# First expert's token rows by comparisons and a product; the largest expert last, with the last norm of all tokens beside it

## The chip, the cores and the metric

One Trainium2 chip, one of its cores. The metric is the device time of one execution in microseconds (us). The kernel before takes 1973.52 us, the median of three runs (1973.03 to 1980.09). Engines are named as in the profile: PE multiplies matrices, PEld loads its weights, DVE works on vectors, ACT applies functions, POOL (GpSimd) and SP issue transfers, and POOL also does some vector work.

## The reference, cut to what matters

A decoder layer on 1024 tokens of 1024 columns: an input projection, a gated mixing unit and a dilated attention beside it, an output projection, a layer norm (its result is `h`), a router that gives each token 4 of 32 experts, the experts, and a last layer norm. The part that the change touches:

```python
logits = hf @ w_router + b_router
top_vals, top_idx = lax.top_k(logits, TOP_K)          # 4 of 32 experts for each token
gates = softmax(top_vals)
# for each expert e, on its tokens xb:
g = minimum(xb @ w_gate[e] + b_gate[e], 7)
u = clip(xb @ w_up[e] + b_up[e], -7, 7)
act = (u + 1) * (g * sigmoid(1.702 * g))
out = (act @ w_down[e] + b_down[e]) * gate            # added to the token's row of y
x = layer_norm(alpha * h + y, ln2_g, ln2_b)
```

## The kernel before, in words

**Front.** Projections, gating and attention run first. Then the output projection goes tile by tile, 8 tiles of 128 tokens: `mix` (L536) gives a tile's rows, `logits` its 32 router values, `route` its four experts. `route` makes the 0/1 rows `sel` with four operations (L606, L608), gets each token's place in its expert's list from a product (L610, L612), picks the four places with four more operations (L622), and writes token number and gate to `table` in DRAM with four indirect writes on POOL's queue (L632). `settle` applies the first norm and stores `h` to `hs` in DRAM; `start` stores the starting value of the last sum to `ys`. Tile t is settled and started during tile t+1; the last two tiles wait until `rank` has sorted the experts by their number of tokens (`perm` L558, `order` L561). `follow` orders their instructions behind that.

**Experts.** Experts are taken by rank, in the order of the list `ORDER`; `CAPS` gives the token slots of each rank (256 for rank 0, 64 for rank 31). Ranks with over 128 slots are wide, the others narrow. The order before begins 0, 30, 15, 29, 1, 28, 14, 27 and ends 6, 18, 9, 17, 7, 16, 8, 31. `fetch` loads the expert's part of `table` (`tg`, L737) on SP's queue and gathers its rows of `hs` (`xg`, L749) on POOL's; `prepare` transposes them on PE (L758). Weights come in twelve pieces of 1 MB (L781, SP's queue, five buffers), each split into a high and a low part by ACT (L120) and DVE (L121), two pieces ahead of PE. SP's order is the program's; other engines' instructions are placed by the scheduler when they are ready in its model, earlier lines first. For each expert PE does gate and up of the first half (4 pieces), then the *down* product of the expert before (4 pieces), then gate and up of the second half. Products are L830 (wide) and L821 (narrow). `finish` transposes back for wide experts (L930), scales by the gate (ACT L931, L923), and adds the rows to `ys` by an indirect accumulating write on POOL's queue (L933). Loads 2 to 6 of the weights wait until the first expert's tokens have come.

**End.** After the last expert the rows of the last norm's scale and shift are spread by PE (L977), a loop handles tokens beyond the slots (none here), and 8 tiles of `ys` are loaded (SP, L1047), normalised in three groups `TAILS` (statistics on DVE for tiles 0 and 2, on ACT for the others; L1068 and L1069 on DVE) and stored (L1070).

Of the kernel before, what the change touches and what calls it, by code (L numbers as in the profile page):

```python
# [21 lines left out]
T = 1024  # L22
D = 1024
# [19 lines left out]
ORDER = [r for n in range(8) for r in (n, 30 - 2 * n, 15 - n, 29 - 2 * n)][:31] + [31]  # L43
# [9 lines left out]
TAILS = [(0, 1), (2, 3, 4), (5, 6, 7)]  # L53
ONDVE = (0, 2)
# [23 lines left out]
def layer(tc, i, out):  # L78
# [9 lines left out]
    table = dp.tile([E * SLOTS, 2], I32, name="table")  # L88

# [9 lines left out]
    ln2 = const("ln2", [P, 2, KT], i["ln2_T"])  # L99
# [3 lines left out]
    ovf = cp.tile([1, 2 * MAXOV + 1], I32, name="ovf")  # L103
# [25 lines left out]
    def left_over(pool, bank):  # L129
# [35 lines left out]
        V.tensor_copy(ovf[:, 2 * MAXOV:2 * MAXOV + 1], pn[:, 0:1])  # L165

# [377 lines left out]
    sels, writes = [], []  # L544

    def rank():
# [11 lines left out]
        V.tensor_scalar(perm[:64], ie[:64], kc[:, 1:2], None, op0=OP.is_equal)  # L558
        po = bank("mm", (P, E))
        TE.matmul(po[:1], ecol, perm[:E], start=True, stop=True)  # L560
        return V.tensor_copy(order, po[:1])  # L561
# [36 lines left out]
    def route(t, x, mu, rs, lg):  # L598
# [6 lines left out]
        sel = A.tile([P, 2, E], BF, name="sel", bufs=2)  # L605
        V.tensor_scalar(sel[:, 0], ie, xf[:, 0:1], None, op0=OP.is_equal)  # L606
        for j in range(1, TOPK):
            V.scalar_tensor_tensor(sel[:, 0], ie, xf[:, j:j + 1], sel[:, 0], op0=OP.is_equal, op1=OP.add)  # L608
# [10 lines left out]
        junk = A.tile([P, E], FT, name="junk", bufs=2)  # L619
        dst = A.tile([P, TOPK], I32, name="dst", bufs=2)  # L620
        for j in range(TOPK):
            V.scalar_tensor_tensor(junk, ie, xf[:, j:j + 1], pp, op0=OP.is_equal, op1=OP.mult,  # L622
                                   accum_out=pos[:, j:j + 1])
        mark = V.scalar_tensor_tensor(dst, xf, float(SLOTS), pos, op0=OP.mult, op1=OP.add)
        g4 = A.tile([P, TOPK], FT, name="g4", bufs=2)
# [14 lines left out]
    def settle(t, x, mu, rs, mark):  # L640
        h = big("pt", 3)
        follow(V.scalar_tensor_tensor(h, x, mu[:, 0:1], ln_g, op0=OP.add, op1=OP.mult), mark)
        V.scalar_tensor_tensor(h, h, rs, ln_b, op0=OP.mult, op1=OP.add)
        S.dma_start(out=hs[t * P:t * P + P], in_=h)
        return h

    def start(t, h, lg, sel, den, mark):
# [9 lines left out]
        y = big("pr", 2)  # L657
# [12 lines left out]
    def settle_all(mark=None):  # L670
        rest = []
        for t, x, mu, rs, lg, sel, den, m in done:
            rest.append((t, settle(t, x, mu, rs, mark or m), lg, sel, den, mark or m))
        for r in rest:
            start(*r)
        done.clear()

    for t in range(NT):
        for step in "ablscdr":
# [14 lines left out]
    settle_all(rank())  # L694
# [14 lines left out]
    with (tc.tile_pool(name="c", bufs=1, reuse_waits="tile") as C,  # L709
# [20 lines left out]
        def fetch(r):  # L730
# [6 lines left out]
            SP.dma_start(out=tg, in_=tv[ds(e, 1), 0:nb].rearrange("a b p c -> p (a b) c"))  # L737
# [5 lines left out]
            for q in range(nb):  # L743
# [6 lines left out]
                                              in_offset=bass.IndirectOffsetOnAxis(ap=k.idx, axis=0))  # L750
# [27 lines left out]
        def load(r, c):  # L778
# [4 lines left out]
            if 1 < len(loads) <= RAWS + 1:  # L783
                tc.add_manual_dep(w.ins, first.ins.name, mybir.DependencyInfo(
# [6 lines left out]
        def downs(r):  # L791

            return (8, 10, 9, 11) if r == ORDER[-1] else (8, 9, 10, 11)

        pieces, ready, loads = [], [], []
        for n, r in enumerate(ORDER + [None]):
            pieces += [(r, c) for c in (0, 2, 1, 3)] if r is not None else []
            pieces += [(ORDER[n - 1], c) for c in downs(ORDER[n - 1])] if n else []
# [98 lines left out]
        def down(b):  # L897
# [3 lines left out]
            for c in downs(b.r):  # L901
# [4 lines left out]
                if c == downs(b.r)[2 if b.r == ORDER[-1] else 0]:  # L906
# [29 lines left out]

        bhl = C.tile([P, 2, D], FR, name="bhl")
# [12 lines left out]
        with tc.manual_schedule(engines={mybir.EngineType.SP}):  # L950
# [3 lines left out]
            prepare(b)  # L954
            last, extra = None, left_over(C, bank)
            for n, r in enumerate(ORDER):
# [11 lines left out]
                gu(b, 1, lambda: (finish(), turn(b, 0)))  # L968
                last, b = b, nxt
            down(last)()  # L970


    ZP = top.enter_context(tc.tile_pool(name="zpsum", bufs=1, space=PSUM))
# [150 lines left out]
```

## Time and profile before

| | us |
|---|---|
| median of three runs | 1973.52 |
| the profiled execution's own time | 1973.29 |
| its span, first to last instruction | 1971.4 |
| PE busy | 1844.5 (94%) |
| DVE busy | 1548.3 (79%) |
| ACT busy | 1315.8 (67%) |

A row of a timeline gives the start (us from the span's start), the duration, engine, line, operation, what is written and read, shapes and how many instructions are merged; in brackets the idle time ahead of it and what ended it. `SPq` and `ACTq` are transfers issued on those queues. A row of the chain of waits gives start, duration, and what the time was spent in.

### The profile page before, as it was taken

The page shows a single profiled execution, that of the slowest core. Times are in us where ns is not written, and L with a number is a line of the kernel's source. Part 1 is how long each engine was busy: PE and PEld are TensorE (multiplying, and loading weights), DVE is VectorE, ACT ScalarE, POOL GpSimd, SP SyncE. Part 2 cuts the span into 40 slices and gives each one's busy share as a digit, 9 for nine tenths or more (in the row PEclk, how much of TensorE's full clock was granted, in tenths as well). Part 3 has the DMA queues.
Part 4 walks back from the last instruction along what each step waited for, and adds up shares of the span by engine and source line. Part 5 has one row for each costly group of instructions (what it writes and reads, how often), then busy time and mean ns, then how long its engine had stood idle before and what let it go on. Part 6 is the DMA issues. An engine that isn't in the chain of part 4 may idle for free.

```text
span 1971.4 us, 32268 instructions
## 1 busy us (share of the span) xinstructions
PE 1844.5 (94%) x12232; PEld 1519.5 (77%) x12232; DVE 1548.3 (79%) x2169; ACT 1315.8 (67%) x1731; POOL 312.1 (16%) x200
## 2 busy tenths in 40 slices
PE   8999998989959999999999999999999999999981
PEld 7687786678747768888887888888888888888861
DVE  5754747667759778778888789898988988989895
ACT  5533526552337677678777778778877887887873
POOL 2111110213330112020111112011111111201110
PEclk9999999989969999999999999999999999999996
DMA  6111101242268898889899899999999999999884
GB/s 202 50 44 35 40 25 36 69 152 97 87 234 317 285 325 305 304 298 371 302 300 351 296 332 322 364 328 317 377 308 334 360 330 348 327 359 348 307 282 176
DMA packets 93054, 495.01 MB, mean 251 GB/s; under 512 B 20880, under 2 KB 21440, under 8 KB 43744
## 3 DMA queue, kind: packets, MB, share of 16 engines
q1 hardware_dynamic: 75856, 442.48, 60.7%
q0 software_dynamic: 14736, 42.04, 8.7%
q10 hardware_dynamic: 2304, 8.39, 1.1%
q8 instruction: 98, 1.61, 0.3%
q14 instruction: 60, 0.49, 0.1%
HBM read 456.59 MB, written 36.27 MB: 250 GB/s over the span
## 4 chain that ended last, share of the span: by engine, by line
PE 53%; DMA 8%; DVE 6%; issue 2%; ACT 2%; POOL 1%; SPq 0%; POOLq 0%; ACTq 0%; DVEq 0%
PE b L830 28%; PE b L821 22%; DMA raw<-in_w_moe 4%; DVE wl L121 3%; DMA ys<-o,tg 3%; PE b L758 2%; ACT wh L120 2%; PE b L930 1%; PE b L844 1%; DVE y L1069 1%; DMA bias<-in_b_guT 0%; DVE y L1068 0%; DMA y<-ys 0%; POOL table L632 0%; DVE tw L867 0%
## 5 line engine op out<-in xcount | busy, mean ns | idle before, releaser
L121 DVE TENSOR_TENSOR wl<-raw,wh 128x2048 bf16<-128x2048 f32 (+1 forms) x385 | 874.8, 2284 | 155.0 <-ACT wh L120 153.6
L120 ACT ACTIVATE wh<-raw 128x2048 fp32r<-128x2048 f32 (+1 forms) x394 | 742.4, 1893 | 153.0 <-DMA raw<-in_w_moe 46.8
L830 PE MATMUL b<-xw,wh 128*128 128x280 f32 (+13 forms) x1920 | 326.4, 324 | 0.0
L830 PEld LDWEIGHTS b<-xw,wh 128*128 128x128 f32 x1920 | 297.8, 190 | 9.5
L821 PE MATMUL b<-wh,xt 128*128 128x512 f32 x1056 | 283.4, 409 | 0.1
L821 PEld LDWEIGHTS b<-wh,xt 128*128 128x128 f32 x1056 | 198.9, 189 | 51.0 <-DVE xt L121 1.0
L830 PEld LDWEIGHTS <-wl 128*128 128x128 bf16 x2880 | 209.0, 97 | 18.1 <-issue 5.1
L749 POOL DMA_INDIRECT xg<-hs,tg x47 | 78.1, 1662 | 743.6 <-PE b L758 264.8
L933 POOL DMA_INDIRECT ys<-o,tg x47 | 110.2, 2344 | 424.8 <-ACT o L931 153.0
L830 PE MATMUL b<-aw,wh 128*128 128x280 f32 (+13 forms) x960 | 160.0, 321 | 0.7 <-DVE aw L121 0.7
L830 PE MATMUL b<-xbw,wl 128*128 128x140 bf16 (+13 forms) x1920 | 153.4, 237 | 2.2 <-DVE wl L121 2.2
L830 PEld LDWEIGHTS b<-aw,wh 128*128 128x128 f32 x960 | 147.7, 188 | 5.5 <-DVE aw L121 0.9
L821 PE MATMUL b<-wh,at 128*128 128x512 f32 x528 | 147.6, 421 | 0.0
L821 PE MATMUL b<-wl,xbt 128*128 128x512 bf16 x544 | 130.1, 382 | 0.0
L865 ACT ACTIVATE sb<-b 128x140 f32<-128x140 f32 (+13 forms) x240 | 71.8, 313 | 79.1 <-PE b L830 72.4
L821 PEld LDWEIGHTS b<-wh,at 128*128 128x128 f32 x528 | 99.9, 192 | 26.2 <-issue 0.6
L821 PEld LDWEIGHTS <-xbt 128*128 128x128 bf16 x544 | 48.0, 98 | 67.6 <-issue 19.5
L867 DVE SCALAR_TENSOR_TENSOR tw<-b,bias,sb 128x140 f32<-128x140 f32 (+13 forms) x240 | 83.8, 389 | 11.3 <-ACT sb L865 10.6
L830 PE MATMUL b<-abw,wl 128*128 128x140 bf16 (+13 forms) x960 | 77.1, 237 | 2.4 <-ACT abw L880 1.7
L124 PE MATMUL mm<-xh,wh 128*128 128x512 f32 x160 | 69.2, 432 | 10.3 <-DVE ks L359 6.9
L821 PE MATMUL b<-wl,abt 128*128 128x512 bf16 x272 | 72.4, 390 | 6.2 <-ACT abt L760 5.7
L124 PE MATMUL mm<-vh,xh 128*128 128x256 f32 x256 | 72.6, 284 | 0.6 <-DVE ql L344 0.6
(364 smaller groups left out, 2804.8 us busy)
## 6 DMA issues: line engine op xcount, KB each, us to landing
raw<-in_w_moe SPq DMA_DIRECT2D x384, 1024.0 KB, 7.2
raw<-in_w_in SPq DMA_DIRECT2D x18, 512.0 KB, 3.7
raw<-in_w_out SPq DMA_DIRECT2D x8, 512.0 KB, 3.5
t<-in_x SPq DMA_DIRECT2D x8, 512.0 KB, 4.2
hs<-pt ACTq DMA_DIRECT2D x8, 512.0 KB, 3.6
ys<-pr ACTq DMA_DIRECT2D x8, 512.0 KB, 2.6
y<-ys SPq DMA_DIRECT2D x8, 512.0 KB, 7.3
out<-y SPq DMA_DIRECT2D x8, 512.0 KB, 2.6
```

Of the source, the lines that this page charges most:

```text
L120: S.activation(hi, src, AF.Copy)
L121: by.tensor_tensor(lo, src, hi.bitcast(FT), op=OP.subtract)
L124: TE.matmul(o, ah, bh, start=start, stop=False)
L749: k.got = G.indirect_dma_start(out=k.x[:k.n], out_offset=None, in_=hs, in_offset=bass.IndirectOffsetOnAxis(ap=k.idx, axis=0))
L758: TE.transpose(tp[:, j], src(j), ident[:n, :n])
L821: TE.matmul(o, a, b, start=first and q == 0, stop=kq == 1 and q == len(every) - 1)
L830: TE.matmul(o, a, b, start=kq == 0 and j == 0, stop=kq == 1 and j == 3)
L844: TE.matmul(p, b.oh, bhl[:, m, half * 512:half * 512 + 512], start=True, stop=False)
L865: S.activation(x2[:, :n], p[f][:, n:2 * n], AF.Copy)
L867: V.scalar_tensor_tensor(t[:, f * n:f * n + n], p[f][:, :n], b.bias[:, c:c + 1], x2[:, :n], op0=OP.add, op1=OP.add)
L930: TE.transpose(tp[:k.n, f], t[:, f, k.q * P:k.q * P + k.n], ident)
L933: G.indirect_dma_start(out=ys, out_offset=bass.IndirectOffsetOnAxis(ap=k.idx, axis=0), in_=k.o[:k.n], in_offset=None, compute_op=OP.add)
```

## The change

- **Order.** Rank 0, the largest, goes last: 1, 30, 15, 29, 2, 28, 14, 27, ... 7, 18, 9, 17, 8, 16, 31, 0.
- **First rows.** The first expert's tokens are no longer read from `table`: `first_rows` picks the expert's places of all 1024 tokens (`place`, one more operation per tile in `route`), compares them with 256 slot numbers (16 comparisons of 128 columns on DVE), and gets the token numbers from products with (1, token base). Its `tg` is loaded later, behind the second and third weight pieces. The first weight load waits for the last store of `hs`. `start` of the last tile follows `first_rows`.
- **Router.** The four operations for `sel` become one broadcast comparison and a reduction, and so do the four for `pos`. The tile before the last is settled during the last one.
- **End.** Before the second half of the last expert its predecessor's rows are written; then the tiles of `ys` are loaded, normalised one by one and stored on POOL's queue beside the last expert's work. The last expert's *down* keeps the tokens in place (`down_last`), adds to its gathered rows of `ys`, and writes the normalised rows over `out` by indirect writes.
- **Scale and shift rows** go to DRAM by 16 small transfers at the very start, and are read back as rows.
- The loop for tokens beyond the slots stands within an outer loop that runs once if there are any, and then all tiles are normalised again.

```diff
-ORDER = [r for n in range(8) for r in (n, 30 - 2 * n, 15 - n, 29 - 2 * n)][:31] + [31]
+ORDER = [r for n in range(7) for r in (n + 1, 30 - 2 * n, 15 - n, 29 - 2 * n)] + [8, 16, 31, 0]
...
-ONDVE = (0, 2)
+ONDVE = (0, 3, 6)
...
-    ln2 = const("ln2", [P, 2, KT], i["ln2_T"])
+        for n in range(2):
+            for k in range(KT):
+                G.dma_start(out=rowd[n:n + 1, k * P:k * P + P].rearrange("n p -> p n"), in_=i["ln2_T"][:, n, k:k + 1])
...
+    def first_rows():
+        pr = bank("po", (P, E))
+        TE.matmul(pr, perm[:E, ORDER[0]:ORDER[0] + 1].to_broadcast([E, P]), ident[:E, :E], start=True, stop=True)
+        own = spare[:, NT * E + 256:2 * NT * E + 256].rearrange("p (t e) -> p t e", t=NT)
+        V.tensor_tensor(own, place, pr.unsqueeze(1).to_broadcast([P, NT, E]), op=OP.mult)
+        at = A.tile([P, NT], FT, name="at")
+        V.tensor_reduce(at, own, axis=AX.X, op=OP.add)
+        for q in range(2):
+            m = big(("kb", "ql0")[q], 1, BF).rearrange("p (t s) -> p t s", t=NT)
+            ps = bank("s", (P, 2))
+            for t in range(NT):
+                V.tensor_scalar(m[:, t], slot[:, q * P:q * P + P], at[:, t:t + 1], None, op0=OP.is_equal)
+                TE.matmul(ps, m[:, t], who[:, t], start=t == 0, stop=t == NT - 1)
+            mark = V.tensor_scalar(rows0[:, q:q + 1], ps[:, 0:1], float(T), ps[:, 1:2], op0=OP.add, op1=OP.add)
+        return mark
...
-        h = big("pt", 3)
+        h = big("pt", 3) if t + 2 < NT else big(f"ks{t + 2 - NT}")
...
-            elif step == "s" and t + 1 < NT:
+            elif step == "s":
                 settle_all()
+                if t + 1 < NT:
+                    start_all()
...
-    settle_all(rank())
+    done[0] = (*done[0][:-1], rank())
+    settle_all()
+    start_all(first_rows())
...
-                                              in_offset=bass.IndirectOffsetOnAxis(ap=k.idx, axis=0))
+                                              in_offset=bass.IndirectOffsetOnAxis(
+                                                  ap=k.idx if r != ORDER[0] else rows0[:k.n, q:q + 1], axis=0))
...
-            if 1 < len(loads) <= RAWS + 1:
-                tc.add_manual_dep(w.ins, first.ins.name, mybir.DependencyInfo(
+            if len(loads) <= RAWS + 1:
+                tc.add_manual_dep(w.ins, (first if len(loads) > 1 else norms[-1]).ins.name, mybir.DependencyInfo(
...
+        def last_norm(b):
+            rows = C.tile([P, 2, D], FT, name="bhl")
+            for n in range(2):
+                G.dma_start(out=rows[:, n], in_=rowd[n:n + 1].to_broadcast([P, D]))
+            ...
+            held = {t: tile_of(t) for t in range(6)}
+            for k in b.parts:
+                G.indirect_dma_start(out=k.y, out_offset=None, in_=ys,
+                                     in_offset=bass.IndirectOffsetOnAxis(ap=k.idx, axis=0))
+            yield
+            for t in range(NT):
+                y = held.pop(t) if t in held else tile_of(t)
+                ...
+                normed(y, y, mv[:, 0:1], rsqrt(C, mv[:, 1:2], 1, "rz"), rows)
+                G.dma_start(out=out[t * P:t * P + P], in_=y)
+                yield
+
+        def down_last(b, step):
+            ...
+                if kq:
+                    for k, p, s in zip(b.parts, ps[half], st):
+                        V.scalar_tensor_tensor(k.y[:, d], p, k.gate, k.y[:, d], op0=OP.mult, op1=OP.add)
+                        V.bn_stats(s[:, half], k.y[:, d])
+                step()
+                step()
+            mv = C.tile([P, 2, 2], FT, name="mv", bufs=3)
+            for k, s in zip(b.parts, st):
+                G.indirect_dma_start(out=ys, out_offset=bass.IndirectOffsetOnAxis(ap=k.idx, axis=0),
+                                     in_=k.y, in_offset=None)
+                V.bn_aggr(mv[:, k.q], s)
+            ...
+            for k in b.parts:
+                z = C.tile([P, D], FT, name="tw", bufs=3)
+                normed(z, k.y, mv[:, k.q, 0:1], rs[:, k.q:k.q + 1], b.rows)
+                G.indirect_dma_start(out=out, out_offset=bass.IndirectOffsetOnAxis(ap=k.idx, axis=0),
+                                     in_=z, in_offset=None, bounds_check=T - 1, oob_is_err=False)
...
+            finish()
+            norms = last_norm(b)
+            next(norms)
+            gu(b, 1, lambda: next(norms))
+            next(norms)
+            next(norms)
+            down_last(b, lambda: next(norms, None))
```

## Rows read from the trace of the kernel before

**Rows 1.** The profile's first part: busy us, share of the span, instructions of each engine.
```profile
PE 1844.5 (94%) x12232; PEld 1519.5 (77%) x12232; DVE 1548.3 (79%) x2169; ACT 1315.8 (67%) x1731; POOL 312.1 (16%) x200
```

**Rows 2.** Stages: length, then PE, PEld, DVE, ACT, POOL busy; clock, DMA share, GB/s.
```profile
555.00:565.00 10.00, 0.00 (x0) 0.00 (x0) 3.84 (x13) 1.91 (x1) 3.21 (x3) 0.50 0.48 134
...
596.70:618.40 21.70, 21.70 (x131) 18.08 (x130) 20.35 (x22) 17.17 (x20) 2.32 (x1) 1.00 0.89 351
...
690.00:800.00 110.00, 105.93 (x567) 82.07 (x566) 87.44 (x75) 80.71 (x83) 18.68 (x8) 0.97 0.91 324
...
1500.00:1600.00 100.00, 99.69 (x728) 83.21 (x727) 87.39 (x87) 83.77 (x103) 16.94 (x8) 1.00 0.97 343
```

**Rows 3.** The chain of waits, 530 to 580 us, and the first expert product (timeline, PE).
```profile
546.09 4.93 POOL table L632
...
561.88 2.60 POOL xg L749
...
564.79 5.27 DMA xg<-hs,tg
...
572.64 5.47 PE L830 MATMUL b<-xw,wh 128*128 128x512 f32 x16
```

**Rows 4.** Timeline of DVE and POOL, 544 to 556 us.
```profile
544.50 0.23 DVE L558 TENSOR_SCALAR perm<-ie,kc 64x32 f32<-64x32 f32 x1
544.81 0.97 POOL L632 DMA_INDIRECT table<-pay,dst  x1 [0.52 <-DVE perm L558]
545.24 2.46 DVE L642 SCALAR_TENSOR_TENSOR pt<-t,mean,tab 128x1024 f32<-128x1024 f32 x2
...
553.60 1.80 POOL L938 MEMSET bhl<- 64x2048 f32 x1
...
555.79 0.29 DVE L776 TENSOR_SCALAR oh<-onesr,perm 128x128 fp32r<-128x128 f32 x1
```

**Rows 5.** The profile's transfers: KB each, median us from issue to landing.
```profile
hs<-pt ACTq DMA_DIRECT2D x8, 512.0 KB, 3.6
```

**Rows 6.** Timeline of POOL and DVE near the start.
```profile
3.14 0.59 POOL L92 DMA_DIRECT2D ln<-in_ln_T  x1
...
16.98 0.42 DVE L307 TENSOR_TENSOR ws<-ws,le 128x256 f32<-128x256 f32 x1 [0.67 <-DMA ws<-in_sgu_wT]
```

**Rows 7.** PE near the end: timeline, and of the chain the row of 128 products.
```profile
1878.63 0.40 PE L844 MATMUL b<-bhl,oh 128*128 128x512 f32 x1
...
1886.47 13.69 PE b L830 x128
...
1903.85 1.91 PE L930 MATMUL b<-ident,tw 128*128 128x128 f32 x16
...
1925.24 1.28 PE L821 MATMUL b<-wh,at 128*128 128x512 f32 x4
```

**Rows 8.** DVE: groups by line, 573 to 640 us; timeline of one reciprocal root.
```profile
L121 DVE TENSOR_TENSOR wl<-raw,wh 128x2048 bf16<-128x2048 f32 x16 | 36.2, 2284 | 7.9 <-ACT wh L120 7.8
L867 DVE SCALAR_TENSOR_TENSOR tw<-b,bias,sb 128x256 f32<-128x256 f32 x16 | 7.0, 478 | 1.7 <-ACT sb L865 1.7
...
L876 DVE SCALAR_TENSOR_TENSOR tw<-tw 128x1024 f32<-128x1024 f32 x2 | 2.4, 1216 | 0.0
...
1950.53 0.16 DVE L108 TENSOR_SCALAR r_y<-var 128x3 int32<-128x3 int32 x1
...
1952.30 1.28 DVE L1069 SCALAR_TENSOR_TENSOR y<-y,r_y,rows 128x1024 f32<-128x1024 f32 x1
```

**Rows 9.** The end: chain of waits, and the timeline of POOL and DVE.
```profile
1907.62 7.36 DMA ys<-o,tg
...
1915.78 6.29 DMA ys<-o,tg
...
1929.04 1.44 POOL L933 DMA_INDIRECT ys<-o,tg  x1 [9.14 <-ACTq L982]
...
1938.20 1.29 DVE L1052 BATCH_NORM_STATS2 st<-y 128x6 f32<-128x512 f32 x2 [10.20 <-DMA y<-ys]
```

More of the change, by code (lines that the diff above doesn't have):

```diff
@@ L98, in layer @@
     ecol = const("ecol", [E, 1], i["c_ecol"])
-    ln2 = const("ln2", [P, 2, KT], i["ln2_T"])
+    with nc.allow_non_contiguous_dma(reason="once, and long before its use"):
+        for n in range(2):
+            for k in range(KT):
+                G.dma_start(out=rowd[n:n + 1, k * P:k * P + P].rearrange("n p -> p n"), in_=i["ln2_T"][:, n, k:k + 1])
+    rows0 = cp.tile([P, 2], I32, name="rows0")
     cnt = cp.tile([64, E], FT, name="cnt")
@@ L542, in follow @@
             mybir.DependencyClass.NoSync, mybir.DependencyReason.SCHED_ONLY), reason="the route first")
-    sels, writes = [], []
+    sels, writes, norms = [], [], []
+    spare = big("va", 2)
+    place = spare[:, 0:NT * E].rearrange("p (t e) -> p t e", t=NT)
+    slot = spare[:, NT * E:NT * E + 256]
+    slot_i = A.tile([P, 256], I32, name="t2", bufs=2)
+    G.iota(slot_i, pattern=[[1, 256]], base=-FAR, channel_multiplier=0)
+    V.tensor_copy(slot, slot_i)
+    who = A.tile([P, NT, 2], BF, name="who")
+    V.tensor_copy(who[:, :, 0:1], tok[:, 0:1].unsqueeze(1).to_broadcast([P, NT, 1]))
+    for t in range(NT):
+        V.memset(who[:, t, 1:2], float(t * P - T))
+    def first_rows():
[13 more added lines that the diff above has]
+        return mark
     def rank():
@@ L604, in route @@
         V.tensor_copy(xf, x8[:, :TOPK])
[L605 to L608, printed above, removed]
+        sel = A.tile([P, 2, E], BF, name="sel", bufs=3)
+        each = spare[:, 2 * NT * E + 256 + t % 2 * TOPK * E:][:, :TOPK * E].rearrange("p (j e) -> p j e", j=TOPK)
+        V.tensor_tensor(each, ie.unsqueeze(1).to_broadcast([P, TOPK, E]), xf.unsqueeze(2).to_broadcast([P, TOPK, E]),
+                        op=OP.is_equal)
+        with nc.allow_low_precision(reason="zeros and ones"):
+            V.tensor_reduce(sel[:, 0], each.rearrange("p j e -> p e j"), axis=AX.X, op=OP.add)
         pp = bank("po", (P, E))
@@ L618, in route @@
         pos = A.tile([P, TOPK], FT, name="pos", bufs=2)
-        junk = A.tile([P, E], FT, name="junk", bufs=2)
         dst = A.tile([P, TOPK], I32, name="dst", bufs=2)
-        for j in range(TOPK):
-            V.scalar_tensor_tensor(junk, ie, xf[:, j:j + 1], pp, op0=OP.is_equal, op1=OP.mult,
-                                   accum_out=pos[:, j:j + 1])
+        V.tensor_tensor(each, each, pp.unsqueeze(1).to_broadcast([P, TOPK, E]), op=OP.mult)
+        V.tensor_reduce(pos, each, axis=AX.X, op=OP.add)
         mark = V.scalar_tensor_tensor(dst, xf, float(SLOTS), pos, op0=OP.mult, op1=OP.add)
+        V.scalar_tensor_tensor(place[:, t], sel[:, 0], -float(FAR), pp, op0=OP.mult, op1=OP.add)
         g4 = A.tile([P, TOPK], FT, name="g4", bufs=2)
@@ L967, in layer @@
                     prepare(nxt)
[L968 to L973, printed above, removed]
-    rows = ZP.tile([P, 2, D], FT, name="rows")
-    for n in range(2):
-        for k in range(KT):
-            TE.matmul(rows[:, n, k * P:k * P + P], ln2[:, n, k:k + 1].to_broadcast([P, P]), ident,
-                      start=True, stop=True)
-    more = nc.values_load(ovf[0:1, 2 * MAXOV:2 * MAXOV + 1], min_val=0, max_val=MAXOV)
```

245 lines of the change are left out of this document (146 added, 99 removed).

## The prediction

> **What bounds the kernel now.** I read the engines' shares first, then the busy time by stage, then the chain of waits at the two ends of the expert stage, then the timelines there. PE is busy 94% of the span and DVE 79% [rows 1]. Among the experts PE hardly rests: 0.3 us in 1500 to 1600, with DVE at 87% and transfers at 0.97; 4.1 us in 690 to 800, where three narrow experts follow each other [rows 2]. So the middle is PE's, with little air on DVE and in the transfers. PE is empty at two places. Between router and first expert it does nothing from 555 to 565 [rows 2]: the chain runs through POOL's table writes, the reading of the table, the gathers at 561.88 and 564.79, and the first product at 572.64 [rows 3]. And after the last product, which ends at 1926.52 [rows 7], 44.9 us of the 1971.4 us span remain: an accumulating write issued at 1929.04, the first tile back on DVE at 1938.20 [rows 9], and 33 us of norms and stores. The change works on both. A measurement of this kernel can tell about 0.5%, 9.9 us, from no change.
>
> **Start.** Fifteen more transfers on POOL at up to 0.59 us each [rows 6] put off its later ones by 8.9 us. The `ws` load is one of these, and DVE's use of it at 16.98 already waits 0.67 us for it [rows 6]. If that instruction keeps its place, DVE, and PE behind it, stand up to 8.2 us; if the scheduler moves it back, nothing happens, since nothing near needs `ws`. I take +1 (0 to +9).
>
> **Seam.** Removed from the path is the wait for the table to land and its reading. What is left ahead of the gathers is rows, POOL and `hs`.
> - DVE: `perm` comes at 544.5 [rows 4]. In its front the router's shorter form saves about 1 us for each of the last two tiles (eight 32-column operations become four; one of that kind takes 0.23 [rows 4]), while settling and starting the tile before the last, now done here, adds about 4: two operations of 1.23 us (half of the pair's 2.46 [rows 4]) and as much again for `start`. So `perm` at 546.5. The last tile's own two take 2.5 (549.0). Then product and reduction over 256 columns, 0.9, sixteen comparisons of 128 columns at 0.2 to 0.29 (the row of that shape is 0.29 [rows 4]) 3.2 to 4.6, two adds 0.4: rows ready at 553.5 to 555.
> - POOL: four writes of the last tile, 0.97 and a gap of 0.30 each [rows 4], 5.1 us from 546.5, and the memset of 1.80 [rows 4], which used to lie under the table's reading, now stands ahead of the gathers. One write took 4.93 instead of 0.97 while DVE ran four wide two-input operations without a pause (545.24 on [rows 3, 4]). Two of the four are gone from here, so I add 1.2. First gather 555, the second 2.9 later as before (561.88 to 564.79 [rows 3]): 557.9, against 564.8.
> - Weights: the first piece now waits for the last `hs` store, issued about 549.3, landing 3.6 later [rows 5], 553. A piece is twice that size, by estimate 7.2: 560, and its split, on ACT and then on DVE, at about DVE's 2.28 each [rows 8], ends at 564.6. The first product comes 7.85 after the second gather [rows 3], at 565.7. So it fits, barely.
>
> I take -7. With POOL never blocked it is -10; with POOL blocked through the comparisons, or the weights 4 us late, -3.
>
> **Order of the experts.** The work is the same. But each group of four has a smaller leader, 92 tokens less in all up to rank 7 (256 to 164), and 16 and 31, both narrow, follow each other. Per token PE needs (21.7 - 13.69)/100 = 0.08 us for four pieces [rows 2, 7], 0.24 for all twelve, so a group is 1 to 9 us shorter on PE with the same 48 MB. With transfers at 0.91 to 0.97 some of it comes back as waits; 690 to 800 shows 4.1 for such a stretch. +2 (-2 to +8).
>
> **End, PE's ledger.** From 572.64 to the first half of rank 31 at 1878.63 [rows 7] PE works and waits 1306.0 us. In the new order what precedes the second half of rank 0 is this, plus *down* of rank 8 (13.69), plus rank 31 (7.8 for each half, 1878.63 to 1886.47, and 7.3 for its *down*), less two stretches of 21.7 [rows 2, 7]; the 1.91 of transposes of rank 8 come in and those of rank 0 drop out. 1306.0 + 13.7 + 22.9 - 43.4 = 1299.2, so this half begins at 1871.8 before the shifts above. Call it t0. About there rank 31's *down* ends.
>
> **End, DVE's ledger.** By the old rows a write is issued 2.5 after the last product, and the first tile is on DVE 11.7 after it [rows 7, 9]; I add 1.8 for POOL's queue: norms begin at t0 + 13.5. From there DVE has:
> - eight tiles, each a reciprocal root of 1.77 (1950.53 to 1952.30) and two passes, 2.5 together [rows 8]: 34.2; statistics of three tiles on DVE, 1.29 and 0.3 each [rows 9]: 4.8; three small operations for each of the other five, 0.6: 3.0. Together 42.0.
> - two weight splits still to come, 4.4; the rest of rank 0's second half: four operations of 0.48, clamp, product and split, 5.0; four additions to `y` with statistics, 0.7 and 0.65 each, 5.4 [rows 8, 9].
>
> That is 56.8 us, while PE needs 29.9 more. So DVE is the bound of the end, and the norms are not hidden but only begun earlier. Behind the last addition come aggregate and root 2.4, two passes 2.5, and two indirect writes to `out` of which the second waits for the first: before, two such writes of one expert stand 8.2 apart, each 6.3 to 7.4 [rows 9]. Those accumulate; a plain store takes 3.6 [rows 5]; I take 5 each, and 1.6 for the loops' exit: 16.5. With 3 for waits of tiles on their loads and on ACT: t0 + 13.5 + 56.8 + 16.5 + 3 = 1961.6, against 1971.4. -10 (bounds below).
>
> **Sum.** +1 - 7 + 2 - 10 = -14: span 1957.4. The profiled execution took 1973.29, 1.9 over its span and 0.2 under the median of the runs. Forecast 1959.
>
> **Rivals.**
> - *PE stays the bound at the end.* If the norms fit between DVE's other work, the end is t0 + 43.4 + 2.7 + 16.5, 27 us earlier: 1932. For it: ACT takes five tiles' statistics. Against: the two ledgers, 56.8 against 29.9. Chance 0.09.
> - *Given back.* Seam -3 by blocked POOL or late weights, end -3 because DVE stands about 7 us more before the first tile (loads beside the weights) or before the late ones: 1970. For it: the seam's three conditions lie within 3 us. Chance 0.25.
> - *POOL becomes the bound of the end: slower.* The loads of tiles 6 and 7 stand in the program behind the stores of tiles 5 and 6, all on POOL's queue. If the scheduler leaves them there, and each store waits for DVE's passes as the write of 4.93 did [rows 3], each of the two tiles costs DVE about 4.9 + 0.6 + 3.6 + 2.8 (wait, issue, load, ACT) = 12 us: +24. With the seam at -3, +28 on the forecast: 1987. It decides once the loads are issued less than 5 us (one tile's work on DVE) before their turn. Against: plain transfers of POOL take 0.59 at the start [rows 6], and the scheduler may move loads forward. Chance 0.08. *The Trainium skill, "SBUF — State Buffer", section "SBUF: two separate sides", says that a transfer issued from GpSimd's queue can't write its descriptors while VectorE holds the port they share, and advises another queue. By that rule every load and store of this end would wait. The row of 4.93 agrees for an indirect write; no row shows a plain one beside such work.*
> - That the change doesn't do what it says would be rows that wait for the table all the same; no line does.
>
> **Chances.** Forecast 0.58, with three quarters of it under 1963.6; rivals as given. Faster: 0.44 + 0.09 = 0.53, said as 0.52; slower 0.08; the same 0.40. The range leaves out the first rival's and the last one's value, 0.17: from start +0, seam -10, between -2 and an end 13 better (1938), to start +9, seam -3, between +5 and an end of -1 (1983).
>
> **What would show it.** Right: the second gather near 558, no table read before it; the first product near 566; DVE without gaps from the first tile's statistics to the last pass, PE idle in short stretches there; two writes to `out` apart by a landing at the very end. Wrong: DVE idle over 5 us in that stretch; POOL's plain transfers of over 2 us; a first x split that waits for DVE at 17; PE idle over 10 us more among the experts.

## The result, and the profile after

Six timed runs of each kernel, taken together, give 1960.0 us (1955.9 to 1965.2) after and 1974.1 (1970.6 to 1980.7) before: a ratio of 0.9928, 95% interval 0.9911 to 0.9946. That is 14 us, 0.7%: faster, and within 1 us of the forecast of 1959. The profiled execution took 1959.75 with a span of 1958.0, 13.4 shorter than before; the prediction's sum was -14. But the terms do not agree with the sum: the start was 12 worse than priced, the order and the end together 13 better.

I cut both spans at the same four places: `perm` (the experts sorted), the first expert product, t0 (the second half of rank 0, or for the kernel before its place in the prediction's ledger), the end.

| stage | before | after | difference | predicted |
|---|---|---|---|---|
| begin to `perm` | 544.50 | 559.67 | +15.2 | +3 (start +1, router and settling +2) |
| `perm` to first product | 28.1 | 20.3 | -7.8 | -9 |
| first product to t0 | 1299.2 | 1294.2 | -5.0 | +2 |
| t0 to end of span | 99.6 | 83.8 | -15.8 | -10 |

The shares of the engines of the kernel after, first part of its page (before: [rows 1]):

```profile
PE 1843.6 (94%) x12086; PEld 1518.0 (78%) x12170; DVE 1558.2 (80%) x2216; ACT 1309.1 (67%) x1729; POOL 339.6 (17%) x238
```

They hardly moved: nothing in this table tells where 13 us went. The stages do. Stages of the kernel after (length, then PE, PEld, DVE, ACT, POOL busy; clock, DMA share, GB/s), near the start and from the first tile's statistics to DVE's last pass:

```profile
8.00:12.00 4.00, 3.25 (x10) 2.03 (x8) 0.47 (x1) 1.06 (x1) 1.04 (x2) 1.00 1.11 151
20.00:25.00 5.00, 4.15 (x19) 3.09 (x17) 1.14 (x1) 1.77 (x2) 1.04 (x2) 1.00 0.81 95
25.00:30.00 5.00, 1.49 (x3) 0.93 (x4) 3.25 (x5) 2.67 (x4) 4.77 (x8) 0.70 0.85 227
...
1891.92:1942.41 50.49, 27.28 (x114) 18.89 (x113) 49.87 (x148) 19.32 (x47) 9.40 (x14) 0.79 0.48 191
```

And the same stages at the start of the kernel before:

```profile
8.00:12.00 4.00, 3.47 (x12) 2.49 (x12) 1.23 (x1) 1.89 (x2) 1.94 (x4) 1.00 1.04 386
20.00:25.00 5.00, 4.73 (x21) 3.60 (x20) 4.32 (x7) 3.55 (x6) 0.00 (x0) 1.00 0.96 347
25.00:30.00 5.00, 5.00 (x24) 4.14 (x23) 1.96 (x2) 0.81 (x1) 0.00 (x0) 1.00 0.61 187
```

The transfer engines are nearly as busy as before (1.11 against 1.04 in 8 to 12, 0.81 against 0.96 in 20 to 25), but they move 151 GB/s instead of 386, then 95 instead of 347; in 25 to 30 PE works 1.5 us of 5. The timeline of the kernel after shows what they were busy with, and then the seam and the end:

```profile
13.38 1.06 POOL L104 DMA_DIRECT2D rowd<-in_ln_T  x2 [3.91 <-DMA rowd<-in_ln_T]
...
22.76 1.06 ACT L126 ACTIVATE xh<-pt 128x1024 fp32r<-128x1024 f32 x1 [4.93 <-DMA pt<-in_xT]
23.62 1.04 POOL L104 DMA_DIRECT2D rowd<-in_ln_T  x2 [6.24 <-DMA rowd<-in_ln_T]
25.13 0.57 POOL L228 DMA_DIRECT2D tab<-in_c_tab  x1 [0.47 <-DMA rowd<-in_ln_T]
...
41.50 0.42 DVE L314 TENSOR_TENSOR ws<-ws,le 128x256 f32<-128x256 f32 x1 [10.92 <-DMA ws<-in_sgu_wT]
43.88 3.64 ACT L350 ACTIVATE qh<-s 64x512 fp32r<-64x512 f32 x6 [3.43 <-PE s L132]
...
559.67 0.23 DVE L593 TENSOR_SCALAR perm<-ie,kc 64x32 f32<-64x32 f32 x1
560.58 1.36 POOL L669 DMA_INDIRECT table<-pay,dst  x1 [0.30 <-issue]
563.24 3.29 DVE L576 TENSOR_SCALAR kb<-va,at 128x128 bf16<-128x128 f32 x8
...
569.15 1.20 POOL L800 DMA_INDIRECT xg<-hs,rows  x1 [0.85 <-DVE lg L687]
577.02 2.34 PE L810 MATMUL b<-ident,xg 92*128 92x92 f32 x12 [2.73 <-DMA xg<-hs,rows]
579.97 1.47 PE L879 MATMUL b<-xw,wh 128*128 128x440 f32 x3 [0.60 <-DVE xw L127]
...
1874.16 3.81 PE L879 MATMUL b<-xw,wh 128*128 128x512 f32 x16
1891.92 1.29 DVE L1016 BATCH_NORM_STATS2 st<-xg 128x6 f32<-128x512 f32 x2 [2.21 <-DMA xg<-ys]
...
1909.46 0.57 POOL L1002 DMA_DIRECT2D xg<-ys  x1 [2.65 <-DMA out<-xg]
...
1939.92 2.48 DVE L988 SCALAR_TENSOR_TENSOR tw<-tw,ry_y,bhl 128x1024 f32<-128x1024 f32 x2
1943.43 1.02 POOL L1069 DMA_INDIRECT out<-tw,tg  x1 [3.17 <-DMA out<-xg]
1948.70 1.01 POOL L1069 DMA_INDIRECT out<-tw,tg  x1 [4.26 <-issue]
```

**Start.** POOL waits for its own small transfers (3.91, 6.24 us), `tab` goes out at 25.13, and ACT gets an x tile at 22.76 after a wait of 4.93; before, that tile came at 16.09. `ws` then holds DVE for 10.92, which is the stall of [rows 6] that the prediction had in mind. Attention's first `qh` starts on ACT at 43.88. In the kernel before it starts 13 us earlier, so most of the 15 us are lost by there:

```profile
30.76 3.64 ACT L343 ACTIVATE qh<-s 64x512 fp32r<-64x512 f32 x6 [4.95 <-PE s L126]
```

How much of the 13 comes by the late x tiles, and how much by POOL's queue (`tab`, `ws`) that stands behind its small transfers, is not separated here.

**Seam** (answers to [rows 3, 4]). The second gather is issued 9.5 after `perm` instead of 20.3, and waits for DVE, not for POOL: the table writes take 0.96 to 1.36 each and are done before the rows are. The first product starts 10.8 behind the second gather, where [rows 3] had 7.85. The gathered tile comes 7.9 after its issue instead of 5.3 (PE waits 2.73 for it), but it is not what ends last. From the comparisons on, the chain of waits of the kernel after runs through no transfer: it goes through `start` of the last two tiles (L699), and behind that through the high and low part of the first weight piece and of the tokens:

```profile
572.94 1.29 DVE vn L699 x2
...
574.63 1.92 ACT wh L126
576.57 2.29 DVE wl L127
578.86 1.06 DVE xw L127 x2
```

e1_direct's chain is the same up to its first product. In the change and in all nine experiments that have the comparisons, PE's use of the second gather begins 17.35 to 17.8 after `perm`, and the first product comes 20.29 to 20.30 after it.

**End** (answers to [rows 7 to 9]). From 1891.92 to 1942.41 DVE is busy 49.87 us of 50.49, PE 27.28. DVE is the bound of this stretch, as the ledger said. But it is 50.5 long, and the prediction had 64.7 for it (56.8, 4.9 and 3).

### The profile page after: what moved, and what is told of

It reads as the page before. It is cut to its first block, busy times and chain, and to the rows that moved or that the text cites. A ratio compares the mean times of both kernels' runs of the same rounds, so it can differ in the third digit from the quotient of the medians.

```text
span 1958.0 us, 32145 instructions
## 1 busy us (share of the span) xinstructions
PE 1843.6 (94%) x12086; PEld 1518.0 (78%) x12170; DVE 1558.2 (80%) x2216; ACT 1309.1 (67%) x1729; POOL 339.6 (17%) x238
## 2 busy tenths in 40 slices
DMA packets 94400, 498.04 MB, mean 254 GB/s; under 512 B 21503, under 2 KB 22047, under 8 KB 45088
## 4 chain that ended last, share of the span: by engine, by line
PE 75%; DVE 8%; DMA 6%; ACT 5%; issue 5%; POOL 0%; POOLq 0%; ACTq 0%; DVEq 0%; SPq 0%
PE b L879 28%; PE b L870 23%; PE mm L130 3%; PE mm L131 3%; PE mm L132 3%; ACT wh L126 3%; DMA raw<-in_w_moe 2%; PE po L405 2%; DVE wl L127 2%; PE b L810 2%; PE tp L396 1%; PE s L131 1%; PE s L130 1%; PE s L132 1%; DMA rowd<-in_ln_T 1%
## 5 line engine op out<-in xcount | busy, mean ns | idle before, releaser
L879 PEld LDWEIGHTS <-wl 128*128 128x128 bf16 x2816 | 203.5, 98 | 16.8 <-issue 6.4
L800 POOL DMA_INDIRECT xg<-hs,tg x45 | 88.8, 1974 | 719.1 <-PE b L810 236.5
L982 POOL DMA_INDIRECT ys<-o,tg x45 | 102.3, 2274 | 386.5 <-ACT o L972 161.5
L879 PE MATMUL b<-aw,wh 128*128 128x280 f32 (+12 forms) x896 | 147.0, 320 | 0.0
L879 PEld LDWEIGHTS b<-aw,wh 128*128 128x128 f32 x896 | 138.1, 192 | 2.1
L870 PE MATMUL b<-wl,xbt 128*128 128x512 bf16 x497 | 124.1, 380 | 2.8
L879 PE MATMUL b<-abw,wl 128*128 128x140 bf16 (+12 forms) x896 | 70.4, 236 | 4.7 <-ACT abw L929 2.5
L132 PE MATMUL mm<-vh,xl 128*128 128x256 f32 x256 | 72.7, 284 | 0.0
```

The source lines that it names most:

```text
L132: TE.matmul(o, al, bh, start=False, stop=stop)
L800: k.got = G.indirect_dma_start(out=k.x[:k.n], out_offset=None, in_=hs, in_offset=bass.IndirectOffsetOnAxis(ap=k.idx if r != ORDER[0] else ...
L870: TE.matmul(o, a, b, start=first and q == 0, stop=kq == 1 and q == len(every) - 1)
L879: TE.matmul(o, a, b, start=kq == 0 and j == 0, stop=kq == 1 and j == 3)
L982: G.indirect_dma_start(out=ys, out_offset=bass.IndirectOffsetOnAxis(ap=k.idx, axis=0), in_=k.o[:k.n], in_offset=None, compute_op=OP.add)
```

## The experiments

In each experiment the time is given as a ratio to the kernel before, measured on the same chip. The intervals are 2 to 4 in 1000 (3 to 8 us) to either side, and single executions of one kernel differ by up to 10 us. In nine kernels that have the new front and no transfers of single values `perm` lies anywhere from 539.9 to 548.8, and the stage from the first product to t0 takes 1294.7 to 1301.0. So small effects are read from the stage of the trace in which they lie, not from the whole time.

### The start: the form of 16 small transfers

**e1_direct**, scale and shift given as two rows:

```diff
...
-                G.dma_start(out=rowd[n:n + 1, k * P:k * P + P].rearrange("n p -> p n"), in_=i["ln2_T"][:, n, k:k + 1])
...
-                G.dma_start(out=rows[:, n], in_=rowd[n:n + 1].to_broadcast([P, D]))
+                G.dma_start(out=rows[:, n], in_=i["ln2"][n:n + 1].to_broadcast([P, D]))
```

> The changed kernel without the 16 small transfers at the start: scale and shift come as an input of two rows, and the last norm reads them from there. Theory 1 (the 16 transfers cost the start its 15.2 us): the sort of the experts (perm), at 559.67 in the changed kernel and 544.50 before, comes back to 544 to 546, the x tiles reach ACT at 8.9 to 22.2 as before, and the time falls by about 15, to 1945. Rival (the transfers are harmless, and the start is late because the scheduler placed the longer program otherwise): perm stays near 559 and the time near 1960.

Ratio 0.9852 (0.9820 to 0.9883), 1948.6 us. That is 0.0076 under the change's ratio, 15 us. `perm` at 548.33, x tiles on ACT at 8.43, 16.14 and 21.95, the first `qh` at 30.93. Theory 1 holds.

**e2_contig**, the same 16 transfers, the same bytes, in runs of 128 values:

```diff
...
-                G.dma_start(out=rowd[n:n + 1, k * P:k * P + P].rearrange("n p -> p n"), in_=i["ln2_T"][:, n, k:k + 1])
+            G.dma_start(out=rowd[n:n + 1, k * P:k * P + P], in_=i["ln2"][n:n + 1, k * P:k * P + P])
```

> The changed kernel with the same 16 transfers at the same place in POOL's queue and of the same bytes, but each copies 128 values that lie side by side on both ends, where the change's take 128 single values. Theory 1a (the form: transfers of single values that land after 9 to 15 us hold up the loads of x): the time is that of the kernel without them, 1945 to 1948, perm at 545 to 547. Theory 1b (the place: 16 issues of 0.53 ahead of the mask, of ws and of the rest on POOL's queue, as the prediction had it): the ws operation still holds DVE up for about 8, perm 551 to 555, time 1952 to 1956.

Ratio 0.9856 (0.9825 to 0.9887), `perm` at 542.47: as without them, so 1a holds. The place in the queue did what the prediction said, and it was still free. Timeline of this kernel, DVE:

```profile
26.70 0.43 DVE L313 TENSOR_TENSOR ws<-ws,le 128x256 f32<-128x256 f32 x1 [7.45 <-DMA ws<-in_sgu_wT]
```

DVE stood 7.45 us for `ws` (the prediction's bound was 8.2), yet attention's first `qh` came at 29.1, where the kernel before had it at 30.8. The x tile that ACT had at 16.09 before came at 12.96; the likely reason, not tested by itself, is that `tab`, 512 KB, was issued at 15.49 instead of 3.71 and left the transfers to the x loads. The issues of this kernel's and of the change's small transfers (KB each, median us to landing); first this kernel's:

```profile
rowd<-in_ln POOLq DMA_DIRECT2D x16, 0.5 KB, 5.0
```

and the change's:

```profile
rowd<-in_ln_T POOLq DMA_DIRECT2D x16, 0.5 KB, 13.3
```

**e3_before_rowd**, the kernel before plus the 16 transfers:

```diff
     ln2 = const("ln2", [P, 2, KT], i["ln2_T"])
...
+                G.dma_start(out=rowd[n:n + 1, k * P:k * P + P].rearrange("n p -> p n"), in_=i["ln2_T"][:, n, k:k + 1])
```

> The kernel before with the 16 transfers of single values added at the place where the change has them, and nothing else; nothing reads what they write. Theory 1: it becomes 13 to 15 slower, 1987 to 1989, with perm at 558 to 560. Rival (another part of the change makes the start late): 1974, perm at 544 to 546.

Ratio 1.0053 (1.0032 to 1.0074), 10 us slower, `perm` at 555.68, 11.2 later, and the first `qh` at 41.35, 10.6 later. Somewhat less than expected, but in the direction and at the place of theory 1: these transfers alone make the start late. In the twelve traces without them at the start `qh` begins at 29.1 to 32.2.

**e12_late**, the change with the same transfers behind the loads of the first norm's rows:

```diff
...
+                w = G.dma_start(out=rowd[n:n + 1, k * P:k * P + P].rearrange("n p -> p n"), in_=i["ln2_T"][:, n, k:k + 1])
+                tc.add_manual_dep(w.ins, g_load.ins.name, mybir.DependencyInfo(
+                    mybir.DependencyClass.NoSync, mybir.DependencyReason.SCHED_ONLY), reason="later")
```

> The changed kernel with the same 16 transfers of single values, put on POOL's queue behind the loads of the first norm's rows (behind attention's last projections) instead of the very start; all else as the change has it. Theory 1 (they cost only because they run beside the x loads that PE waits for): perm 542 to 548 as without them, time 1945 to 1950, ratio 0.985 to 0.988. Rival (such transfers hold up whatever runs beside them, so the front pays at the later place too): perm 552 to 560, time 1953 to 1960.

The rival holds: ratio 0.9903 (0.9881 to 0.9925), `perm` at 553.47. They go out at 402 to 420, land after 8.0 to 13.0, and now the output projection's x tile, loaded on SP's queue, is the one that waits. Timelines of this kernel:

```profile
419.87 0.52 POOL L516 DMA_DIRECT2D rowd<-in_ln_T  x1 [3.94 <-DMA rowd<-in_ln_T]
...
433.09 1.06 ACT L535 ACTIVATE t<-t 128x1024 f32<-128x1024 f32 x1 [12.45 <-DMA t<-in_x]
```

Without them (e1_direct) that tile comes at 427.70:

```profile
427.70 1.06 ACT L528 ACTIVATE t<-t 128x1024 f32<-128x1024 f32 x1 [5.01 <-DMA t<-in_x]
```

In all traces but e12_late's this wait is 3.3 to 5.6. So it is not the start that is special; there was no harmless place among the two that were tried. The loss here is 10 us against e1_direct, where the change loses 15.

The Trainium skill, "DMA: Bandwidth & Descriptors", section "Rules for kernel authors", says that a last dimension that is not contiguous becomes one descriptor for each element, and advises to rearrange. The runs agree with the advice: the same 8 KB in runs cost nothing that the times can tell, in single values 10 to 15 us, and the kernel paid in the loads beside them. The number of descriptors is not shown by the traces: they count 512 packets more for the 16 transfers in both forms (94400 in the change and in e2_contig, 93888 in e1_direct).

### The seam: rows by comparisons

**e4_table**, based on e1_direct, reads the rows from the table again:

```diff
-                                                  ap=k.idx if r != ORDER[0] else rows0[:k.n, q:q + 1], axis=0))
+                                                  ap=k.idx, axis=0))
...
-    start_all(first_rows())
+    start_all()
```

> The kernel without the 16 transfers, with the first expert's rows read from the table again (no comparisons, no product, no place per token, its list loaded at once, the first weight load not held back). The earlier settling and the shorter router stay. Theory 2 (the rows by comparisons are the seam's gain): from perm to the first product it takes about 28 again instead of 20.3, and the time is 8 above that of the kernel without the transfers, about 1953. Rival (the gain comes from the earlier settling and the shorter router, which leave POOL's writes unblocked): perm to first product 21 to 24, time 1946 to 1949.

Timeline of this kernel:

```profile
545.73 0.23 DVE L588 TENSOR_SCALAR perm<-ie,kc 64x32 f32<-64x32 f32 x1
556.57 0.40 SPq L778 DMA_DIRECT2D tg<-table  x1
559.61 2.42 POOL L793 DMA_INDIRECT xg<-hs,tg  x1 [7.20 <-issue]
562.33 1.20 POOL L793 DMA_INDIRECT xg<-hs,tg  x1 [0.30 <-issue]
...
572.22 4.00 PE L872 MATMUL b<-xw,wh 128*128 128x440 f32 x10
```

`perm` to first product 26.5, against 20.3 in e1_direct and e2_contig alike, and 28.1 before. So the rows give 6.2 of the 7.8, and against the kernel before 1.6 are left for the earlier settling and the rest. (e8_before_order, with the old seam and the first expert of the new order, takes 30.3; against it they are 3.8.) The list is read 10.8 after `perm`, behind the last table write, and the chain of waits runs through the second gather (7.8 to its use) as it did before. The ratio, 0.9896 (0.9866 to 0.9926), is 0.0044 above e1_direct's, 9 us, as expected though within the two intervals.

### The order

**e8_before_order**, the kernel before with one line changed:

```diff
-ORDER = [r for n in range(8) for r in (n, 30 - 2 * n, 15 - n, 29 - 2 * n)][:31] + [31]
+ORDER = [r for n in range(7) for r in (n + 1, 30 - 2 * n, 15 - n, 29 - 2 * n)] + [8, 16, 31, 0]
```

> The kernel before with the new order of the experts alone (rank 0 last, 1 first); its seam, its end and its start stay. The prediction's ledger puts 1299.2 between the first product and the second half of rank 0, and took +2 for waits; the changed kernel showed 1294.2. Theory 6 (the order itself is what saves the 5): 1293 to 1296 here as well. Rival (the saving comes from another part, such as the first list of tokens that is read later): 1299 to 1303. The whole time ends with a wide expert's write and all eight norms behind it, so 1970 to 1985, and says little.

First product at 576.83, t0 at 1873.66: 1296.8. Between the two expectations, but the eleven other traces with this order lie at 1294.2 to 1301.0, mean 1296.9. So the order alone gives what the whole change gives in this stage, about -2.3 against the ledger; the -5.0 of the change's own profile is one draw of that spread. The ledger is one draw too: e3_before_rowd, with the old order, gives 1300.0 by the same sum. A shift of 2 to 3 is small against a spread of 7 us, so that the order saves time in this stage is likely, but not shown. The whole time is 0.9980 (0.9963 to 0.9997).

### The end: what DVE pays, who issues, how it closes

**e5_roots**, based on e1_direct:

```diff
+                rsqrt(C, mv[:, 1:2], 1, "rx")
                 normed(y, y, mv[:, 0:1], rsqrt(C, mv[:, 1:2], 1, "rz"), rows)
```

> The kernel without the 16 small transfers, and in the norms beside the last expert each of the eight tiles computes its reciprocal root twice (the first result is unused). Nine more small operations per tile. Theory 3 (DVE bounds the end, and a small operation that alternates with other work costs 0.065 to 0.07 us): 72 times 0.07, 5 more, about 1953. As the prediction priced it (1.77 for each root, DVE the bound): 14 more, about 1962. Rival (PE or the loads bound the end): 0 to 1 more, 1948 to 1949.

From the first tile's statistics to DVE's last pass: 55.3, against 50.5 to 52.8 (mean 51.8) in six traces without the second root (the change, e1_direct, e2_contig, e4_table, e6_nodep, e9_noloop). So eight more roots of nine operations cost 3.5, 0.05 an operation: theory 3. At the price of the prediction they would have cost 14. Timeline of DVE in this kernel, where operations of two roots and others alternate:

```profile
1906.35 0.15 DVE L111 TENSOR_TENSOR rz_w<-rz_y 128x1 f32<-128x1 f32 x1
1906.42 0.15 DVE L1020 TENSOR_SCALAR mv<-mv 128x1 f32<-128x1 f32 x1
1906.49 0.15 DVE L112 TENSOR_TENSOR rx_w<-rx_w,mv 128x1 f32<-128x1 f32 x1
1906.55 0.15 DVE L112 TENSOR_TENSOR rz_w<-rz_w,mv 128x1 f32<-128x1 f32 x1
```

They start 0.06 to 0.07 apart. The nine operations of [rows 8], each of which needs the one before, took 1.77, 0.2 apart. The ratio, 0.9896 (0.9859 to 0.9933), can't tell 3.5 from 14.

**e6_nodep**, based on e1_direct:

```diff
...
+                if wrote:
+                    tc.declare_no_dep(zw.ins, wrote[-1].ins.name, reason="other tokens")
```

> The kernel without the 16 small transfers, in which the second of the two last indirect writes (tokens of the last expert over the output) no longer waits for the first; the two write different tokens. Theory 4 (the two landings stand one after the other at the very end): the second is issued 1.0 behind the first instead of 4.2, and the time falls by 3.2, to about 1945. Rival (the exit of the loops, which runs beside the landing, hides it): the same time, 1948.

Timeline of POOL in this kernel:

```profile
1935.59 1.02 POOL L1065 DMA_INDIRECT out<-tw,tg  x1 [3.18 <-DMA out<-xg]
1936.91 1.01 POOL L1065 DMA_INDIRECT out<-tw,tg  x1 [0.30 <-issue]
```

First write to the end of the span: 13.3 (1935.59 to 1948.9), against 16.1 to 17.0 in e1_direct, e2_contig, e4_table and e5_roots. The second write goes out 1.3 behind the first instead of 4.2, and from it to the end it takes 12.0, within the 11.9 to 12.8 of those four. So the 3 are there, theory 4. (The change itself has 14.6 and e7_actq 14.3 with the wait in place, because their close is shorter; see e9_noloop.) The times can't show them: 0.9877 (0.9839 to 0.9914).

**e7_actq**, based on e1_direct:

```diff
-                G.dma_start(out=y, in_=ys[t * P:t * P + P])
+                S.dma_start(out=y, in_=ys[t * P:t * P + P])
...
-                G.dma_start(out=out[t * P:t * P + P], in_=y)
+                S.dma_start(out=out[t * P:t * P + P], in_=y)
```

> The kernel without the 16 small transfers, with the loads of the eight tiles of the last norm and their stores issued on ACT's queue instead of POOL's. By the prediction's rival (POOL's transfers are held back while DVE works without a pause) and the page behind it the norms would begin and end earlier: 5 or more off the time, 1943 or less. Theory 5 (POOL issues these transfers in 0.54 to 0.58, unblocked, and DVE bounds the end): within 2 of the kernel without the small transfers, 1946 to 1950, or later by what ACT's order puts ahead of a store.

Ratio 0.9906 (0.9869 to 0.9943): no gain, rather a loss. The norms begin 17.0 after t0 instead of 17.8, but take 59.0 instead of 51.8. DVE's waits in that stretch of this kernel:

```profile
DVE st L1011 <- DMA xg<-ys: 5.0, 1, 5.0
DVE wl L122 <- ACT wh L121: 2.9, 1, 2.9
DVE st L1011 <- DMA xt<-ys: 1.1, 1, 1.1
```

In the change the same stretch has 2.2 and 0.3 of such waits, and POOL issues each plain transfer there in 0.53 to 0.58 while DVE is busy 99% of the time. So the prediction's rival fell: POOL's issues were not held up, and ACT's queue was not the better one. The prediction read the section that it set beside this rival too widely. The Trainium skill, "SBUF — State Buffer", section "SBUF: two separate sides", ties starved descriptors to operations of DVE in a 2-port performance mode, and says that one with two inputs in SBUF contends with a GpSimd instruction that reads SBUF, not with one that only writes it. The wide passes of this stretch have two inputs in SBUF, and issues of 0.53 to 0.58 beside them agree with that. This run is no clean test of the queue alone, since on ACT's queue a load or store also stands in the order of ACT's own work.

**e9_noloop**, based on e1_direct, ends behind the last expert:

```diff
-    with tc.For_i(0, some, 1):
-        with tc.For_i(0, more, 1) as j:
...
```

> The kernel without the 16 small transfers and without what follows the last expert: the two loops that would handle tokens beyond the slots and norm all tiles again are left out (this input has no such tokens, so nothing else changes). Theory 7 (behind the landing of the last write the engines leave the loops for about 8.8, where the prediction took 1.6): the span ends within 1 of that landing, first of the last two writes to the end 8 instead of 16 to 17, time 1940 to 1941. As the prediction priced it: 1947.

A miss. From the last write to the end it takes 8.4 (1945.71 to 1954.1) instead of 12.1 in e1_direct, so the loops cost 3.7 against that kernel; with 3.2 of landing, 5 remain. But the close behind the landing differs between kernels that all have the loops: 6.0 in the change and e12_late, 7 to 9.5 in the others. So the loops cost about 1 to 4, and no more can be said. SP's waits at the end of this kernel:

```profile
SPq L1160 <- DMA out<-tw,tg: 8.1, 1, 8.1
SPq L1160 <- PEq L1160: 4.6, 2, 4.1
```

After the landing SP waits 4.1 for PE's sequencer at the program's last line. In the kernel before that wait is 0.5. Why it is longer here was not found. The ratio, 0.9867 (0.9850 to 0.9883), shows no gain over e1_direct.

**e10_actstats**, based on e6_nodep:

```diff
-ONDVE = (0, 3, 6)
+ONDVE = ()
```

> The kernel without the 16 small transfers and without the wait between the last two writes, with the statistics of all eight tiles on ACT (tiles 0, 3 and 6 were on DVE). Theory 3 (DVE bounds the end, ACT is half idle there): DVE loses three times 1.4 and gains three times 0.2, norms' begin to last pass 48 to 49 instead of 51 to 53, time 3 to 4 less, 1943 to 1944. Rival (the first tile's statistics take 2.6 on ACT ahead of everything, and the last tiles wait for ACT): 0 to 3 later, 1947 to 1950.

Norms' begin to DVE's last pass 49.9; from t0 to that pass 67.4, against 68.2 to 70.4 (mean 69.5) in the change, e1_direct, e2_contig, e4_table, e6_nodep and e9_noloop. DVE is busy 46.9 us there instead of 49.9 in e6_nodep, so the 3 are off its work; in the gaps it waits 3.3 for ACT's statistics of the first tile and 1.5 for a weight part of ACT's, where e6_nodep waits for loads and PE. What is left is 2 rather than 3 to 4, from one trace, 0.6 below the shortest of the six. The time is 1945.2 us, ratio 0.9852 (0.9835 to 0.9869): the lowest median here, and like e1_direct clearly below the change.

**e11_pool**, based on e6_nodep, for tiles 0 to 5:

```diff
-                normed(y, y, mv[:, 0:1], rsqrt(C, mv[:, 1:2], 1, "rz"), rows)
...
+                    S.activation(y, y, AF.Identity, scale=rs, bias=mv[:, 7:8])
+                    V.tensor_tensor(y, y, rows[:, 0], op=OP.mult)
+                    G.tensor_tensor(y, y, rows[:, 1], op=OP.add)
```

> The kernel without the 16 small transfers and without the wait between the last two writes, in which tiles 0 to 5 of the last norm are scaled and shifted by three engines: ACT subtracts the mean and multiplies by the root, DVE multiplies by the scale row, POOL adds the shift row (2.4 each by POOL's rows in the front). DVE loses six passes of 1.2. Theory 3 (DVE bounds the end): norms' begin to last pass 45 to 46 instead of 51 to 53, time 6 less, about 1941. Rival (POOL's additions beside DVE slow DVE or hold up POOL's loads of tiles 6 and 7): no gain or later, 1947 to 1955.

The rival: norms' begin to last pass 58.7 instead of 51.8, ratio 0.9895 (0.9879 to 0.9912). Timeline of DVE and POOL in this kernel:

```profile
1898.96 0.74 DVE L1056 SCALAR_TENSOR_TENSOR o<-b,tg,o 128x512 f32<-128x512 f32 x1
1898.99 2.40 POOL L1031 TENSOR_TENSOR xg<-xg,bhl 128x1024 f32<-128x1024 f32 x1 [0.92 <-DVE rz_w L115]
1899.62 1.79 DVE L116 SCALAR_TENSOR_TENSOR rz_w<-rz_w,mv 128x1 f32<-128x1 f32 x1
...
1906.62 2.41 POOL L1031 TENSOR_TENSOR xt<-xt,bhl 128x1024 f32<-128x1024 f32 x1 [1.17 <-DVE rz_y L114]
1907.13 1.91 DVE L115 TENSOR_TENSOR rz_w<-rz_y 128x1 f32<-128x1 f32 x1
```

A DVE operation of one column, 0.15 elsewhere, takes 1.79 and ends when POOL's addition ends (1901.41 and 1901.39); the next case is 1.91, again to POOL's end. Beside each of the six additions one small operation is held so, for 1.8 to 2.3 us. The operation at 1898.96 has one input in PSUM and runs its 0.74 beside POOL. About 2 us lost for each addition is more than the pass of 1.2 that it saved. Here the same section of the Trainium skill agrees: it says that an operation of DVE with two inputs in SBUF and one of GpSimd that reads SBUF exclude each other for their whole length. Five of the six operations that were held have two inputs in SBUF; the sixth, a shift of integers, has one.

## Why the prediction was right, and where it was wrong

The time was right, and it fell because of the seam and the end, as forecast; that the sum came out to the microsecond is luck, because the misses cancelled.

**Start, +1 (0 to +9): wrong, +15.** The failed step is "fifteen more transfers on POOL at up to 0.59 us each put off its later ones by 8.9 us". I counted what the transfers cost the queue that issues them and nothing of what they cost the transfer engines. The issue is indeed 0.53. But each is 128 single values, takes 12 to 15 us to land, and while 16 of them are under way the loads of x crawl. e2_contig takes the two apart: with the queue's delay alone (`tab` at 15.49; in the change 25.13) `ws` stalls DVE by 7.45, as priced, and nothing is lost; with the single values the loss is 15. The +2 for the router and the settling does not show either: in the nine traces with the new front and no single values `perm` comes at 545.3 in the mean, before at 544.5 and in e8_before_order at 546.6. No row of before showed a transfer of single values whose landing I had read, so this needed a bound from both sides, and it got one from the issue alone.

**Seam, -7 (-10 to -3): the size right, the path not.** `perm` to first product -7.8. The reading of the table left the path, as said, and POOL's writes were not blocked, so the second gather came 9.5 after `perm` where I had 11.4. But the prediction put the gather last and had the weights "fit, barely", 18.1 after `perm`. In the trace the weights' path ended last: ACT could not begin the first piece's high part before 574.63, behind DVE's `start` of the last two tiles, which the prediction did not have on this path, and the low part was done 19.2 after `perm`. The comparisons are worth 6.2 (e4_table).

**Order, +2 (-2 to +8): about -2, at the edge of its bounds.** e8_before_order shows the order alone at the mean of the other traces; the waits that the +2 stood for did not come.

**End, -10 (-23 to -1 in the prediction's range): -15.8, inside it.** The engine that bounds it was the right one, DVE, busy 49.87 of 50.49, and the first rival (PE the bound) fell with it. Three terms were mis-sized:
- The reciprocal root, 1.77 each. That row is a chain of operations that wait for each other, with DVE otherwise empty. Beside other work the scheduler puts other operations between them, and a root costs 0.45 (e5_roots). Eight times 1.3 is 10.6 of the 14.2 by which the stretch was shorter than priced; of the 3 put down for waits 0.6 came, which is 2.4 more.
- Begin of the norms, t0 + 13.5: it was 17.8. The write of rank 31 was issued at t0 + 7, took 3.27 on POOL, and the first load of a tile went out 3.52 after that, when it had landed.
- Behind DVE's last pass, 11.6: it was 15.6. The first write went out 1.0 after the pass, the second 5.3 behind it, about as priced, and landed after 3.3 instead of 5, but the close after the landing took 6.0 instead of 1.6. It is 6 to 9.5 in the kernels with the loops, 5 without.

**POOL as the bound of the end: fell.** The loads of tiles 6 and 7 did stand behind the stores (1909.46 is one), which was the rival's first condition, but were issued in 0.57 and 0.53, and DVE waited 0.3 for tiles after the first.

**Given back, 1970: fell** at the seam and at the end; what was given back was given back at the start.

The biggest cost of this change is thus a detail that has nothing to do with its idea: without it the same idea gives 1.5% instead of 0.7%.

## What to carry to other kernels

Price a transfer by its landing and by what runs beside it, not by its issue: 8 KB in single values cost 15 us here, in runs nothing, and moved to another place still 10. A chain of small operations costs its latency only where the engine has nothing else; inside a busy stretch count 0.05 to 0.07 for each, not the duration of the chain. Where two paths are said to fit barely, look which one ended last: at the seam it was not the one that had been priced as the last. And when a forecast hits the time, add up the stages all the same: here a start 12 worse than priced, and an order and an end 13 better, hid in a sum that was right.

## What the runs showed of the hardware that I had not expected

- Transfers of 128 single values of 4 bytes, DRAM to DRAM, 0.5 KB each, landed after 8 to 15 us, and beside them the traffic of all queues fell from 386 to 151 GB/s at a busy share of 1.11 instead of 1.04.
- Small DVE operations start 0.2 us apart when each needs the last one's result, and 0.06 to 0.07 apart when they alternate with others.
- A 0.15 us operation of DVE took 1.8 to 2.3 beside each of six additions on POOL, to the end of that addition (e11_pool).
- After the last landing the program's close waited 4.1 (e9_noloop) to 8.0 us (e2_contig) for PE's sequencer, 0.5 in the kernel before. PE had been idle for over 30 us in all of them, so that is not the difference; it stays open.
